# A mixer layer on one core: the Gelu of u held behind the decay chain's last Exp, the gate normalised in pairs, modulation sums called in other slots

## The chip, the cores and the metric

The kernel runs on one core of a Trainium2 chip. Time is device microseconds (us) from one execution of the whole program; lower is better. The engines are TensorE (PE, matmuls; its weight loads are listed as PEld), VectorE (DVE), ScalarE (ACT), GpSimd (POOL) and SyncE (SP, which issues most of the loads). Each engine runs its own list of instructions strictly in order, and waits at an instruction until what it needs is there.

## The reference

One layer over 512 tokens of width 1024, with 256 tokens of context. A wide projection gives u, vs, q, r, ga, gb, k, v and a low-rank input of the decay. Cut to what the change touches:

```python
u, vs, q, r, ga, gb, k, v, lr = _split(h @ w_in, IN_SPLITS)
# spatial gating: vs is layer-normalised over its 1024 channels, mixed over chunks of 128 tokens in 8 groups
a = gelu(u) * (einsum('gpq,bnqgc->bnpgc', w_s, layer_norm(gelu(vs))) + b_s)
# gated linear attention, both directions, 4 heads, chunks of 64 tokens
la = log_sigmoid(lr @ w2 + b2) / 16
b = cumsum(la)            # within a chunk
q_dec, k_inv, k_dec = q * exp(b), k * exp(-b), k * exp(b_last - b)
o = o * rsqrt(mean(o * o) + EPS)      # per head, over 256 channels
ob = o * gla_norm_g * silu(r)
merged = sigmoid(ga) * (a @ w_br_a) + sigmoid(gb) * (ob @ w_br_b)
x = x + g1 * (merged @ w_o)
...                       # then a gated feed-forward block with a 3x3 convolution
```

The vectors g1, sh2, sc2 and g2, by which branches are scaled and shifted, are products of silu(c) with a matrix (w_ada).

## The kernel before

**Matmuls.** Everything is float32. A product is done as three matmuls of rounded halves: high x high, high x low, low x high. A weight comes by DMA into a "raw" tile; ACT's rounding copy makes its high half wh (L152 for whole weights, L232 for sums of weights, whose source is called tt), DVE's subtraction makes its low half wl (L153, L233). Activations are split the same way (L398, L399). Most 128x512 matmuls are at L406 (columns of w_in) and L492 (below).

**Stages, in order, with their place in the profiled execution:** context and heads 0 to 2 (to 189 us); the "u units" (189 to 261); the products VS (vs, 261 to 301), GA (ga, 301 to 353), br_a (a @ w_br_a, 353 to 397), GB (gb, 397 to 438), R (r, 438 to 478), br_b (478 to 531), W_o (531 to 573); the feed-forward part (573 to 931).

**The u units.** For j = 0 to 7, 24 matmuls (L406) give one 128-channel block u_j in a PSUM bank, and `A.activation(ug[j], ps, AF.Gelu)` (L1249) empties it. In each unit `u_slot()` is called twice; it runs the next piece of the attention of heads 2 and 3 (`hook()`). For the last head these pieces are, in order, the decay step `step_z(3)`, the output of head 2 with the sums of its squares (L1050, tiles called junk, read from PSUM banks of the pool "gl"), then `step_transpose` (L978 transposes the context's decayed k, which DVE made at L960; L986 those of the latents), scores, states and outputs.

**step_z.** ACT moves the decay's projections out of PSUM (L912, L880); log-sigmoid is an Exp (L923, for the context L888) and a Ln with bias 1 (L925, L889); DVE makes the running sums over chunks (L931, L892); ACT takes the Exps (L943 to L945, for the context L894); DVE multiplies them with q and k (L956, L957, L960). Where ACT turns from one set of functions to another, the compiled program has an ACT_TABLE_LOAD.

**Strassen products.** `strassen` (from L482) does each of VS, GA, GB, R and W_o as seven half-size products named a11, s3, s2, a12, s1, a22 and s4, of two steps each: 14 slots of 12 matmuls (L492). Between products ACT copies PSUM pairs (L501 after a11, L506 after s3, L510 after s2), and DVE adds pairs (L511, L522). The `step` function that it is given is called once in each slot and puts other work there.

**The gate.** After VS, statistics of gelu(vs) give a scale and an offset for each token; eight ACT instructions (L1287, Identity with bias and scale, 128x512 each) apply them to the eight tiles vr. In GA's step function `ga_step`, `sgu_part(j)` does four small matmuls (L1337) into a bank of the pool "mm", DVE adds the bias (L1339) and multiplies with u_j (L1342); `a_split` then splits u_j for br_a. The two PSUM pools, mm and gl, have four banks each, handed out in turn.

**Modulation sums.** `ada2` is a generator that `tick()` advances; a first group gives g1 and sh2, a second one sc2. Rows of w_ada come in (tiles wa, 256 KB each, on SP's queue), DVE adds them into accumulators (L1307), and at the end of a group a pair of matmuls with ones (L1315, L1316) sums each accumulator over the partitions. In GB, `o_scale` calls `tick()` in each slot.

**What sets the order.** The program is written as one sequence; a scheduler lays it out on the engines by dependencies and its own estimates. `behind(start, name)` (L93) adds an order-only dependency: all instructions traced since `start` come after the one called `name`.

Of the kernel before, what the change touches and what calls it, by code (L numbers as in the profile page):

```python
# [12 lines left out]
AF = mybir.ActivationFunctionType  # L13
# [20 lines left out]
def backbone_kernel(  # L34
# [6 lines left out]
    nc = tc.nc  # L41
    V, A, G, T = nc.vector, nc.scalar, nc.gpsimd, nc.tensor
# [11 lines left out]
    def nm(s):  # L54
        cnt[0] += 1
        return f"{s}_{cnt[0]}"

    def heap(shape, dt=F32, s="h"):
        return hp.tile(shape, dt, tag="h", name=nm(s))
# [18 lines left out]
    def traced():  # L78
        return nc.cur_bb.bb.instructions
# [13 lines left out]
    def behind(start, name):  # L93
        for i in traced()[start:]:
            tc.add_manual_dep(i, name, mybir.DependencyInfo(
                mybir.DependencyClass.NoSync, mybir.DependencyReason.DATA), reason="behind")

    def table_for(func):
        name = [i.name for i in traced() if i.engine == nc.scalar.engine][-1]
        start = len(traced())  # L100
        A.preload_act_table(func)
        behind(start, name)
# [213 lines left out]
    def weights(lead=1, ahead=AHEAD):  # L316
        i = pos[2]
        pos[2] += 1
        stream_split(i + 1 + lead)
        stream_load(i + 1 + ahead)  # L320
        return splits.pop(i)
# [60 lines left out]
    def tick(n=1):  # L382
        for _ in range(n):
            while bg:
                try:
                    next(bg[0])
                    break
                except StopIteration:
                    bg.pop(0)
# [92 lines left out]
    def strassen(acts, done, step, low_first=False):  # L482

        def prod(ps, name, again):
            for j in range(2):
                wh, wl = weights(3, 6)
                for t in range(2):
                    for kk in range(2):
                        ah, al = acts(name, 2 * j + kk, t)
                        first = j == 0 and kk == 0 and not again  # L490
                        for i, (a, b) in enumerate(((ah, wh), (ah, wl), (al, wh))):
                            T.matmul(ps[t], a, b[:, kk, :], start=(first and i == 0),  # L492
                                     stop=(j == 1 and kk == 1 and i == 2), skip_group_check=again)
                step()

        pair = lambda pool: [pool() for _ in range(2)]
        a = pair(mm)
        prod(a, "a11", False)
        b = pair(gl)
        for t in range(2):  # L500
            A.copy(b[t], a[t])  # L501
        e = pair(mm)
        prod(e, "s3", False)
        es = [heap([P, 512], s="es") for _ in range(2)]
        for t in range(2):
            A.copy(es[t], e[t])  # L506
        prod(b, "s2", True)
        c = pair(gl)
        for t in range(2):
            A.copy(c[t], b[t])  # L510
            V.tensor_tensor(b[t], b[t], es[t], op=ALU.add)  # L511

        def c11():
            prod(a, "a12", True)
            for t in range(2):
                done(0, t, a[t], 1.0)

        if not low_first:
            c11()
        prod(c, "s1", True)  # L520
        for t in range(2):
            V.tensor_tensor(es[t], c[t], es[t], op=ALU.add)  # L522
            done(1, 2 + t, es[t], -1.0)
        prod(b, "a22", True)
        for t in range(2):
            done(0, 2 + t, b[t], 1.0)
        if low_first:
            c11()
        prod(c, "s4", True)
        for t in range(2):  # L530
            done(1, t, c[t], -1.0)
# [264 lines left out]
    for k in range(KT):  # L796
# [10 lines left out]
        n = 0  # L807
# [62 lines left out]
    def zc_head(h):  # L870
        S_ = heads[h]
        bcol, wz = gate_col(h)
        zc = gl()
        for d in range(2):
            T.matmul(zc[:, d * LC:(d + 1) * LC], wz[d], lrc, start=True, stop=True)

        lm = wp.tile([P, 4, LC], F32, tag="raw", name=nm("lm"), bufs=5)
        l, m = lm[:, 0:2, :], lm[:, 2:4, :]
        for d in range(2):
            A.activation(l[:, d, :], zc[:, d * LC:(d + 1) * LC], AF.Abs, bias=bcol[d])  # L880
        for d in range(2):
            V.tensor_scalar(m[:, d, :], zc[:, d * LC:(d + 1) * LC], bcol[d], 0.0, op0=ALU.add, op1=ALU.min)
        S_["zc"] = l, m

    def zc_tail(h):
        S_ = heads[h]
        l, m = S_.pop("zc")
        A.activation(l, l, AF.Exp, scale=-1.0)  # L888
        A.activation(l, l, AF.Ln, bias=one_t)  # L889
        for d in range(2):  # L890
            r = slice(None, None, -1 if d == 0 else 1)
            V.tensor_tensor_scan(m[:, d, r], m[:, d, r], l[:, d, r], 0.0, op0=ALU.add, op1=ALU.subtract)  # L892
            G.memset(l[:, d, LC - 1:LC] if d == 0 else l[:, d, 0:1], 1.0)
            A.activation(l[:, d, d:LC - 1 + d], m[:, d, 1 - d:LC - d], AF.Exp, scale=1.0 / 16)  # L894
        S_["ec"] = l
# [5 lines left out]
    def zx_head(h):  # L901
        S_ = heads[h]
        bcol, wz = gate_col(h)
        zx = []
        for d in range(2):
            z = gl()
            T.matmul(z, wz[d], lrx, start=True, stop=True)
            zx.append(z)
        lx, mx = [], []
        for d in range(2):  # L910
            l_ = heap([P, 4, P], s="lx")
            A.activation(l_, zx[d], AF.Abs, bias=bcol[d])  # L912
            m_ = heap([P, 4, P], s="mx")
            V.tensor_scalar(m_, zx[d], bcol[d], 0.0, op0=ALU.add, op1=ALU.min)
            lx.append(l_)
            mx.append(m_)
        S_["zx"] = lx, mx
# [32 lines left out]
    def step_decay(h):  # L950
        S_ = heads[h]
        kx, qx, kc = kxs.pop(h), qxs.pop(h), kcs.pop(h)
        v4 = lambda ap: ap.rearrange("p (i t) -> p i t", i=4)
        S_["q"], S_["k"] = [], []
        for d in range(2):
            V.tensor_tensor(S_["ek"][d], v4(kx), S_["ek"][d], op=ALU.mult)  # L956
            V.tensor_tensor(S_["eq"][d], v4(qx), S_["eq"][d], op=ALU.mult)  # L957
            S_["k"].append(S_["ek"][d])
            S_["q"].append(S_["eq"][d])
        V.tensor_tensor(S_["ec"], S_["ec"], kc.unsqueeze(1).to_broadcast([P, 2, LC]), op=ALU.mult)  # L960

    def mm3(ps, a, b, start, stop):
        for z, (p_, q_) in enumerate(((a[0], b[0]), (a[0], b[1]), (a[1], b[0]))):
            T.matmul(ps, p_, q_, start=(start and z == 0), stop=(stop and z == 2))  # L964

    def step_z(h):
        zx_head(h)
        zc_head(h)
        zx_tail(h)
        zc_tail(h)  # L970
        step_decay(h)

    def step_transpose(h):
# [253 lines left out]
    slots = [0]  # L1227

    def u_slot():
        slots[0] += 1  # L1230
        n = slots[0]
        hook()
        if n == 8:
            sgu_load()
        if n > 8:
            next(summing)
        if n in (11, 13):
            sgu_turn((n - 11) // 2)

    ug = []  # L1240
    for j in range(KT):
        w = weights()
        ps = (mm if j < 3 else gl)()
        for k in range(KT):
            prod_k(ps, w, hx, k, 0, S)
            if k == 3:
                u_slot()
        ug.append(heap([P, S], s="ug"))
        A.activation(ug[j], ps, AF.Gelu)  # L1249
        u_slot()  # L1250
    for low in s3_low:
        low()

    vraw = [[None] * 4 for _ in range(2)]
# [27 lines left out]
    vrs, ors = var[:, 0, :], var[:, 1:5, :]  # L1282
    vnb = const([P, 4], "vnb")
    V.scalar_tensor_tensor(vnb, mv[:, :, 0], -1.0, vrs, op0=ALU.mult, op1=ALU.mult)
    for hf in range(2):
        for t in range(4):
            A.activation(vraw[hf][t], vraw[hf][t], AF.Identity, bias=vnb[:, t:t + 1], scale=vrs[:, t:t + 1])  # L1287

    bc_g = {}
    cols = {}  # L1290
# [53 lines left out]
    def a_split():  # L1344
        a_act.append(split_act(ug[len(a_act)], s="a", eng=A.copy))
# [8 lines left out]

    def ga_step():
        slots[0] += 1
        n = slots[0] - 5
        if 0 <= n < KT:
            sgu_part(n)
        if n >= KT:  # L1360
            a_split()

    strassen(of_sums, ga_done, ga_step)
    slots[0] = 0

    def br_a_done(hf, t, ps):
# [36 lines left out]
    scale_todo = [(t, hf) for hf in range(2) for t in (0, 1, 2, 3)]  # L1403

    def o_scale():
        if scale_todo:
            t, hf = scale_todo.pop(0)
            os_[t][hf] = late([P, 512], s="os")
            for q in range(2):
                h = 2 * hf + q  # L1410
                A.mul(os_[t][hf][:, q * 256:(q + 1) * 256], o_tok[h][t // 2][:, t % 2, :], ors[:, h, t:t + 1])
        tick()

    strassen(of_sums, gb_done, o_scale)
    ada_bank[0] = gl

# [513 lines left out]
    for t in range(2):  # L1930
# [5 lines left out]
        start = len(traced())  # L1936
# [55 lines left out]
```

## Time and profile before

| | |
|---|---|
| median of 3 runs | 933.89 us (933.57 to 934.73) |
| the profiled execution | 932.99 us, of which 931.3 from its first to its last instruction |
| mean granted clock of PE | 0.990 |
| PE, DVE, ACT, POOL busy | 898.0, 766.6, 490.6, 72.0 us |
| HBM read | 135.52 MB |

In the rows of the profile a line reads: start, duration, engine, source line, operation, output<-inputs, shape, how many; in brackets the idle time of the engine before it and what ended that. Rows of stretches give for each engine its busy time in the stretch and the number of instructions that touch it. L-numbers are lines of the kernel before; the changed kernel has the same statements some lines lower (L1249 is L1257 there, L1287 is L1298, L492 is L495).

### The profile page before, as it was taken

The page shows a single profiled execution, that of the slowest core. Times are in us where ns is not written, and L with a number is a line of the kernel's source. Part 1 is how long each engine was busy: PE and PEld are TensorE (multiplying, and loading weights), DVE is VectorE, ACT ScalarE, POOL GpSimd, SP SyncE. Part 2 cuts the span into 40 slices and gives each one's busy share as a digit, 9 for nine tenths or more (in the row PEclk, how much of TensorE's full clock was granted, in tenths as well). Part 3 has the DMA queues.
Part 4 walks back from the last instruction along what each step waited for, and adds up shares of the span by engine and source line. Part 5 has one row for each costly group of instructions (what it writes and reads, how often), then busy time and mean ns, then how long its engine had stood idle before and what let it go on. Part 6 is the DMA issues. An engine that isn't in the chain of part 4 may idle for free.

```text
span 931.3 us, 12864 instructions
## 1 busy us (share of the span) xinstructions
PE 898.0 (96%) x4647; PEld 754.1 (81%) x4647; DVE 766.6 (82%) x1324; ACT 490.6 (53%) x858; POOL 72.0 (8%) x108
## 2 busy tenths in 40 slices
PE   7999999996999799999989999999999999999996
PEld 5777899986888688878868878988888888888885
DVE  5667686876986597888995798799999888999796
ACT  5156464678465762365652568633333343366573
POOL 3000000000121100111111010000000000123000
PEclk9999999998999899999999999999999999999998
DMA  9950401202867548969869074254534333399512
GB/s 271 338 153 1 137 24 46 69 23 78 200 133 206 114 157 258 329 148 305 226 202 226 25 180 138 70 157 130 163 115 125 102 108 108 87 236 261 139 68 91
DMA packets 128093, 138.46 MB, mean 149 GB/s; under 512 B 7401, under 2 KB 84533, under 8 KB 128029
## 3 DMA queue, kind: packets, MB, share of 16 engines
q1 hardware_dynamic: 115933, 117.85, 40.6%
q0 software_dynamic: 10368, 18.57, 11.9%
q10 hardware_dynamic: 1728, 1.22, 0.4%
q8 instruction: 36, 0.59, 0.3%
q14 instruction: 28, 0.23, 0.1%
HBM read 135.52 MB, written 2.10 MB: 148 GB/s over the span
## 4 chain that ended last, share of the span: by engine, by line
PE 78%; DVE 8%; DMA 6%; ACT 5%; issue 1%; SPq 0%; ACTq 0%; POOL 0%; DVEq 0%; POOLq 0%
PE mm L406 27%; PE gl L492 8%; PE gl L1775 6%; PE mm L492 5%; PE mm L1775 4%; PE mm L437 4%; PE mm L430 4%; PE gl L406 4%; DMA wa<-in_w_ada_dram 3%; PE mm L421 2%; PE mm L737 2%; PE gl L964 2%; DMA tt<-in_w_in_dram 2%; PE gl L737 1%; DVE acc L1307 1%
## 5 line engine op out<-in xcount | busy, mean ns | idle before, releaser
L152 ACT CAST wh<-raw 128x1024 fp32r<-128x1024 f32 x110 | 114.3, 1051 | 125.0 <-PE mm L406 67.8
L153 DVE TENSOR_TENSOR wl<-raw,wh 128x1024 fp32r<-128x1024 f32 x110 | 133.3, 1220 | 24.6 <-ACT wh L152 22.2
L1658 DVE SCALAR_TENSOR_TENSOR cacc<-ca,ccol,cacc 128x441 f32<-128x441 f32 (+2 forms) x176 | 121.0, 694 | 6.1 <-ACT cacc L1646 2.8
L406 PE MATMUL mm<-h2h,wh 128*128 128x512 f32 x320 | 124.5, 389 | 0.0
L406 PE MATMUL mm<-h2l,wh 128*128 128x512 f32 x320 | 124.5, 389 | 0.0
L406 PE MATMUL mm<-h2h,wl 128*128 128x512 f32 x320 | 124.5, 389 | 0.0
L406 PEld LDWEIGHTS mm<-h2l,wh 128*128 128x128 f32 x320 | 60.1, 188 | 12.5
L406 PEld LDWEIGHTS mm<-h2h,wh 128*128 128x128 f32 x320 | 60.1, 188 | 12.5
L406 PEld LDWEIGHTS mm<-h2h,wl 128*128 128x128 f32 x320 | 60.1, 188 | 12.3
L232 ACT CAST wh<-tt 128x512 fp32r<-128x512 f32 x60 | 35.4, 620 | 34.8 <-DVE tt L245 15.9
L1307 DVE SCALAR_TENSOR_TENSOR acc<-wa,c_col,acc 128x512 f32<-128x512 f32 x64 | 45.4, 746 | 8.5 <-DMA wa<-in_w_ada_dram 8.3
L1661 ACT ACTIVATE cacc<-cacc 128x512 f32<-128x512 f32 x22 | 13.9, 633 | 61.0 <-DVE cacc L1658 60.9
L233 DVE TENSOR_TENSOR wl<-tt,wh 128x512 fp32r<-128x512 f32 x60 | 39.7, 684 | 5.9 <-ACT wh L232 5.8
L208 POOL DMA_DIRECT2D tt<-in_w_in_dram x32 | 27.5, 927 | 159.4 <-DMA tt<-in_w_in_dram 66.6
L492 PE MATMUL mm<-wh,hxh 128*128 128x512 f32 x96 | 38.0, 395 | 0.0
L492 PE MATMUL mm<-wh,hxl 128*128 128x512 f32 x96 | 37.4, 389 | 0.0
L492 PE MATMUL mm<-wl,hxh 128*128 128x512 f32 x96 | 37.4, 389 | 0.0
L492 PE MATMUL gl<-wh,xh 128*128 128x512 f32 x64 | 26.5, 415 | 5.0 <-ACT gl L501 4.8
L1697 POOL DMA_DIRECT2D b<-in_ffn_w_down_dram x11 | 10.1, 939 | 271.0 <-DMA b<-in_ffn_w_down_dram 257.4
L1717 ACT CAST wh<-raw 128x1024 fp32r<-128x1024 f32 x22 | 23.0, 1052 | 15.3 <-PE mm L1775 4.4
L1718 DVE TENSOR_TENSOR wl<-raw,wh 128x1024 fp32r<-128x1024 f32 x22 | 26.8, 1219 | 4.5 <-ACT wh L1717 4.3
L492 PE MATMUL gl<-wl,xh 128*128 128x512 f32 x64 | 25.5, 399 | 0.0
(534 smaller groups left out, 2461.1 us busy)
## 6 DMA issues: line engine op xcount, KB each, us to landing
raw<-in_w_in_dram SPq DMA_DIRECT2D x54, 512.0 KB, 5.2
wa<-in_w_ada_dram SPq DMA_DIRECT2D x96, 256.0 KB, 5.8
raw<-in_ffn_w_up_dram SPq DMA_DIRECT2D x44, 512.0 KB, 3.9
raw<-in_ffn_w_down_dram SPq DMA_DIRECT2D x22, 512.0 KB, 3.4
tt<-in_w_in_dram POOLq DMA_DIRECT2D x32, 256.0 KB, 6.9
tt<-in_w_in_dram SPq DMA_DIRECT2D x16, 256.0 KB, 4.9
raw<-in_w_br_a_dram SPq DMA_DIRECT2D x8, 512.0 KB, 3.5
raw<-in_w_br_b_dram SPq DMA_DIRECT2D x8, 512.0 KB, 5.3
```

Source lines behind the costliest of these rows:

```text
L152: A.copy(wh, raw)
L153: low = lambda: V.tensor_tensor(wl, raw, wh.bitcast(F32), op=ALU.subtract)
L232: A.copy(wh[:, kk, :], tt[j][kk])
L233: V.tensor_tensor(wl[:, kk, :], tt[j][kk], wh[:, kk, :].bitcast(F32), op=ALU.subtract)
L406: T.matmul(ps, a[:, k, :], b[:, c0:c0 + n], start=(k == 0 and i == 0), stop=(k == KT - 1 and i == 2))
L430: T.matmul(ps, a[:, t * P:(t + 1) * P], b[:, k % 4, :], start=(k == 0 and i == 0), stop=(k == KT - 1 and i == 2))
L437: T.matmul(ps, a, b[:, k % 2, :], start=(k == 0 and i == 0), stop=(k == KT - 1 and i == 2))
L492: T.matmul(ps[t], a, b[:, kk, :], start=(first and i == 0), stop=(j == 1 and kk == 1 and i == 2), skip_group_check=again)
L737: T.matmul(fps[i], a, b, start=(k == 0 and z == 0), stop=(k == KT - 1 and z == 2))
L1307: V.scalar_tensor_tensor(a_, w_, c_col[:, k:k + 1], a_, op0=ALU.mult, op1=ALU.add)
L1658: V.scalar_tensor_tensor(o, a_[:, r0 + dy:r1 + dy, c0 + dx:c1 + dx], wcol(tap), o, op0=ALU.mult, op1=ALU.add)
L1775: T.matmul(ps, a[:, t * P:(t + 1) * P], w[b][:, j, c0:c0 + n], start=(first and i == 0), stop=(last and i == 2), skip_group_check=again)
```

## The change

1. In `step_z` the name of ACT's last instruction so far, the context's last Exp, is kept in `last_exp`. The Gelu of each u_j gets an order-only dependency on it, and the second `u_slot()` of a unit is called ahead of the Gelu. For heads before the last, the dependency is on an Exp that is long past.
2. The eight normalisations leave their place after VS. `vs_norm(i)` does two of them, behind ACT's latest instruction; `ga_step` calls it in slots 3 to 6. `sgu_part` comes one slot later (slots 6 to 13 in place of 5 to 12), `a_split` in slot 14 and once after GA.
3. `o_scale` calls `tick()` in GB's slots 1 to 4 and 9 to 12 alone.

```diff
@@ -95,8 +95,11 @@
             tc.add_manual_dep(i, name, mybir.DependencyInfo(
                 mybir.DependencyClass.NoSync, mybir.DependencyReason.DATA), reason="behind")
 
+    def last_of(engine):
+        return [i.name for i in traced() if i.engine == engine.engine][-1]
+
     def table_for(func):
-        name = [i.name for i in traced() if i.engine == nc.scalar.engine][-1]
+        name = last_of(nc.scalar)
         start = len(traced())
         A.preload_act_table(func)
         behind(start, name)
@@ -963,11 +966,14 @@
         for z, (p_, q_) in enumerate(((a[0], b[0]), (a[0], b[1]), (a[1], b[0]))):
             T.matmul(ps, p_, q_, start=(start and z == 0), stop=(stop and z == 2))
 
+    last_exp = [None]
+
     def step_z(h):
         zx_head(h)
         zc_head(h)
         zx_tail(h)
         zc_tail(h)
+        last_exp[0] = last_of(nc.scalar)
         step_decay(h)
 
     def step_transpose(h):
@@ -1245,9 +1251,11 @@
             prod_k(ps, w, hx, k, 0, S)
             if k == 3:
                 u_slot()
+        u_slot()
         ug.append(heap([P, S], s="ug"))
+        start = len(traced())
         A.activation(ug[j], ps, AF.Gelu)
-        u_slot()
+        behind(start, last_exp[0])
     for low in s3_low:
         low()
 
@@ -1282,9 +1290,13 @@
     vrs, ors = var[:, 0, :], var[:, 1:5, :]
     vnb = const([P, 4], "vnb")
     V.scalar_tensor_tensor(vnb, mv[:, :, 0], -1.0, vrs, op0=ALU.mult, op1=ALU.mult)
-    for hf in range(2):
-        for t in range(4):
-            A.activation(vraw[hf][t], vraw[hf][t], AF.Identity, bias=vnb[:, t:t + 1], scale=vrs[:, t:t + 1])
+
+    def vs_norm(i):
+        name, start = last_of(nc.scalar), len(traced())
+        for t in (2 * (i % 2), 2 * (i % 2) + 1):
+            v_ = vraw[i // 2][t]
+            A.activation(v_, v_, AF.Identity, bias=vnb[:, t:t + 1], scale=vrs[:, t:t + 1])
+        behind(start, name)
 
     bc_g = {}
     cols = {}
@@ -1354,13 +1366,16 @@
 
     def ga_step():
         slots[0] += 1
-        n = slots[0] - 5
+        n = slots[0] - 6
+        if -3 <= n <= 0:
+            vs_norm(n + 3)
         if 0 <= n < KT:
             sgu_part(n)
         if n >= KT:
             a_split()
 
     strassen(of_sums, ga_done, ga_step)
+    a_split()
     slots[0] = 0
 
     def br_a_done(hf, t, ps):
@@ -1403,14 +1418,17 @@
     scale_todo = [(t, hf) for hf in range(2) for t in (0, 1, 2, 3)]
 
     def o_scale():
+        slots[0] += 1
         if scale_todo:
             t, hf = scale_todo.pop(0)
             os_[t][hf] = late([P, 512], s="os")
             for q in range(2):
                 h = 2 * hf + q
                 A.mul(os_[t][hf][:, q * 256:(q + 1) * 256], o_tok[h][t // 2][:, t % 2, :], ors[:, h, t:t + 1])
-        tick()
-
+        if slots[0] < 5 or 8 < slots[0] < 13:
+            tick()
+
+    slots[0] = 0
     strassen(of_sums, gb_done, o_scale)
     ada_bank[0] = gl
```

The following rows are the engines' instruction lists, before and after; the number behind a tile's name tells its buffers apart.

ACT in the u units, before: from the load ahead of the second unit's Gelu to the first squares. lx, mx and lm are the decays of the latents (two directions) and of the context, dec their values at the chunks' ends, ug a Gelu result, junk the squares of head 2's output:

```order
L1249 ACT_TABLE_LOAD
L1249 ACTIVATE ug_2481<-mm_2456 128x512
L943 ACT_TABLE_LOAD
L943 ACTIVATE dec_2417<-dec_2417 128x4
L944 ACTIVATE mx_2395<-lx_2393 128x512
L943 ACTIVATE dec_2429<-dec_2429 128x4
L944 ACTIVATE mx_2399<-lx_2397 128x512
L945 ACTIVATE lx_2393<-lx_2393 128x512
L945 ACTIVATE lx_2397<-lx_2397 128x512
L889 ACT_TABLE_LOAD
L889 ACTIVATE lm_2404<-lm_2404,one_t 128x512
L1050 ACTIVATE junk_2494,oss<-gl_2483 128x256
```

After, from the first Exp of the sums to the first squares:

```order
L946 ACTIVATE dec_2415<-dec_2415 128x4
L947 ACTIVATE mx_2393<-lx_2391 128x512
L892 ACTIVATE lm_2402<-lm_2402,one_t 128x512
L948 ACTIVATE lx_2391<-lx_2391 128x512
L946 ACTIVATE dec_2427<-dec_2427 128x4
L947 ACTIVATE mx_2397<-lx_2395 128x512
L897 ACTIVATE lm_2402<-lm_2402 128x255
L948 ACTIVATE lx_2395<-lx_2395 128x512
L897 ACTIVATE lm_2402<-lm_2402 128x255
L1257 ACT_TABLE_LOAD
L1257 ACTIVATE ug_2448<-mm_2308 128x512
L1056 ACTIVATE junk_2492,oss<-gl_2481 128x256
```

The Gelu and the loads are gone from between the Exps; one load stands behind the last Exp (the second L897), and the squares, which stood ahead of the last Exp, stand behind it and behind the first Gelu.

ACT in GA, before, from the first copy of a11's pair (L501) to the first copy of s3's pair (L506); "..." leaves out five like rows of vr:

```order
L501 COPY gl_3451<-mm_3404 128x512
L232 CAST wh_3460<-tt_3317 128x512
L1287 ACTIVATE vr_3232<-vr_3232,vnb,var 128x512
L1287 ACTIVATE vr_3235<-vr_3235,vnb,var 128x512
...
L1287 ACTIVATE vr_3284<-vr_3284,vnb,var 128x512
L501 COPY gl_3452<-mm_3405 128x512
L152 CAST wh_3480<-raw_3412 128x1024
L506 COPY es_3496<-mm_3455 128x512
```

After, from the second copy (L504) on:

```order
L504 COPY gl_3444<-mm_3397 128x512
L1298 ACTIVATE vr_3232<-vr_3232,vnb,var 128x512
L1298 ACTIVATE vr_3235<-vr_3235,vnb,var 128x512
L155 CAST wh_3474<-raw_3404 128x1024
L1298 ACTIVATE vr_3334<-vr_3334,vnb,var 128x512
L1298 ACTIVATE vr_3337<-vr_3337,vnb,var 128x512
L509 COPY es_3492<-mm_3447 128x512
L155 CAST wh_3496<-raw_3429 128x1024
L509 COPY es_3493<-mm_3448 128x512
L1298 ACTIVATE vr_3378<-vr_3378,vnb,var 128x512
L1298 ACTIVATE vr_3381<-vr_3381,vnb,var 128x512
L155 CAST wh_3516<-raw_3344 128x1024
```

The second copy has moved ahead of the normalisations, which stand in pairs between weight halves (L155) and copies (L509).

DVE in GA, before, from the first low half of a12's weight on:

```order
L153 TENSOR_TENSOR wl_3481<-raw_3412,wh_3480 128x1024
L1339 SCALAR_TENSOR_TENSOR mm_3518<-mm_3518,vec_b,sgb_2686 128x512
L153 TENSOR_TENSOR wl_3501<-raw_3437,wh_3500 128x1024
L1342 TENSOR_TENSOR ug_2387<-mm_3518,ug_2387 128x512
L153 TENSOR_TENSOR wl_3526<-raw_3344,wh_3525 128x1024
L1339 SCALAR_TENSOR_TENSOR mm_3543<-mm_3543,vec_b,sgb_2686 128x512
L511 TENSOR_TENSOR gl_3451<-gl_3451,es_3496 128x512
L1342 TENSOR_TENSOR ug_2481<-mm_3543,ug_2481 128x512
L511 TENSOR_TENSOR gl_3452<-gl_3452,es_3497 128x512
```

After:

```order
L156 TENSOR_TENSOR wl_3475<-raw_3404,wh_3474 128x1024
L156 TENSOR_TENSOR wl_3497<-raw_3429,wh_3496 128x1024
L156 TENSOR_TENSOR wl_3517<-raw_3344,wh_3516 128x1024
L514 TENSOR_TENSOR gl_3443<-gl_3443,es_3492 128x512
L514 TENSOR_TENSOR gl_3444<-gl_3444,es_3493 128x512
L1351 SCALAR_TENSOR_TENSOR mm_3536<-mm_3536,vec_b,sgb_2684 128x512
L156 TENSOR_TENSOR wl_3550<-raw_3364,wh_3549 128x1024
L1354 TENSOR_TENSOR ug_2448<-mm_3536,ug_2448 128x512
```

Two more low halves and both sums (L514, before L511) now stand ahead of the first bias addition (L1351, before L1339).

PE in GB, before, the first pair with ones:

```order
L492 MATMUL gl_4228<-wl_4199,xh_2876 128x512
L492 MATMUL gl_4228<-wh_4198,xl_2877 128x512
L1315 MATMUL mm_4311<-acch_4191,ones_r 128x512
L1316 MATMUL mm_4311<-accl_4192,ones_r 128x512
L492 MATMUL gl_4227<-wh_4236,xh_2958 128x512
```

After:

```order
L495 MATMUL gl_4333<-wl_4312,xh_2874 128x512
L495 MATMUL gl_4333<-wh_4311,xl_2875 128x512
L1327 MATMUL mm_4402<-acch_4191,ones_r 128x512
L1328 MATMUL mm_4402<-accl_4192,ones_r 128x512
L495 MATMUL gl_4332<-wh_4338,xh_2956 128x512
```

The pair stands some 48 matmuls further on; gl_4228 and gl_4333 are PSUM banks of two different products.

## Prediction

> **What bounds the kernel now.** I read the busy shares first, then the waits of TensorE (PE), then the granted clock around its long waits, then the timelines of ScalarE (ACT) and VectorE (DVE) just ahead of them.
>
> ```profile
> span 931.3 us, 12864 instructions
> PE 898.0 (96%) x4647; PEld 754.1 (81%) x4647; DVE 766.6 (82%) x1324; ACT 490.6 (53%) x858; POOL 72.0 (8%) x108
> ```
>
> PE is busy for 898.0 of 931.3 us and the change takes no matmul away, so it can pay only in PE's waits and in the slow clock that follows them. The waits by what ended them, for 185 to 262 us and then for 262 to 600 us (columns: total, times, longest):
>
> ```profile
> PE gl L978 <- DVE lm L960: 7.1, 1, 7.1
> ...
> PE gl L492 <- ACT gl L501: 4.8, 1, 4.8
> ...
> PE mm L1315 <- ACT es L506: 0.9, 1, 0.9
> ```
>
> The first lies in the u units, the second in the product GA, the last in GB. Each part of the change sits just ahead of one of the three; the two rows left out are waits at the head of br_b, which it leaves alone. The clock around the two long waits (the number behind POOL's count is the granted clock):
>
> ```profile
> 218.00:222.00 4.00, 1.97 (x9) 1.98 (x10) 0.74 (x2) 3.96 (x9) 0.00 (x0) 0.50 0.00 0
> 222.00:226.00 4.00, 4.00 (x19) 3.41 (x19) 2.81 (x4) 4.00 (x6) 0.00 (x0) 0.84 0.55 144
> ...
> 318.00:322.00 4.00, 3.90 (x11) 3.22 (x12) 1.23 (x1) 4.00 (x7) 0.00 (x0) 0.50 0.53 92
> ```
>
> [...] In the u units that costs 2 us x 0.5 + 4 us x 0.16 = 1.6 us on top of the 7.1.
>
> **Part 1, the Gelu of u behind the decay chain.** In the u units ACT is the engine that is late. First its whole stretch, then its rows and DVE's:
>
> ```profile
> 196.90:219.20 22.30, 16.00 (x88) 13.48 (x86) 14.31 (x37) 22.09 (x38) 0.20 (x2) 0.94 0.00 1
> 205.90:219.98 14.08, 9.49 (x25) 0.87 0.00 0
> ...
> 196.99 1.28 ACT L1249 ACT_TABLE_LOAD   x1
> 198.29 0.60 ACT L1249 ACTIVATE ug<-mm 128x512 f32<-128x512 f32 x1
> 205.16 1.34 ACT L925 ACTIVATE lx<-lx,one_t 128x512 f32<-128x512 f32 x2
> 216.31 0.37 ACT L1050 ACTIVATE junk<-gl 128x256 bf16<-128x256 f32 x1
> 216.67 0.38 ACT L1050 ACTIVATE junk<-gl 128x256 bf16<-128x256 f32 x1
> 212.51 0.39 PE L406 MATMUL mm<-hxh,wl 128*128 128x512 f32 x1
> 220.03 1.11 PE L978 MATMUL gl<-ident,lm 128*128 128x128 f32 x4 [7.13 <-DVE lm L960]
> ```
>
> ACT is busy for 22.09 of the 22.30 us that end with the last Exp (L894). Nine table loads stand in the u units, of 1.28 us each; the changed order has one. Eight of them, 10.3 us, lie ahead of the last Exp. Three loads (3.85 us) and a Gelu stand ahead of the Ln pair (L925), so that pair starts at 205.16 - 3.85 - 0.5 = 200.8; I take 201.6, since the projections ahead of it (L912, L880) wait for PE and DVE. Its first half is done at about 202.3. From there DVE carries the chain: in the stretch from its first scan to the end of L960 it has 9.49 us of work, so L960 ends at about 202.3 + 9.5 = 211.8. PE comes to L978 right behind the L406 that starts at 212.51, at about 212.7. So the 7.13 us wait goes whole, with 0.9 us to spare, and the half clock with it.
>
> What is late next is the squares of the head before (L1050), which stand behind the one load and the first Gelus in the new order. They read the PSUM banks that L978, L986 and the fourth unit's matmuls want. ACT's last Exp ends at about 209.4 (it runs some 2.3 us ahead of L960, whose inputs L956 and L957 DVE still has to make); then the load (1.30 from its row to the next), two Gelus (0.60 less the overlap, 0.5 each), four squares (0.36 each from start to start) and one wh copy (0.94, from rows in part 2) end at 209.4 + 1.3 + 1.0 + 1.45 + 0.95 = 214.1, and the bank is free at about 214.2. PE has ten transposes to do from 212.74 (four took 1.11 us at half clock, so by an estimate ten take 1.3 at full clock), and so wants the bank at 214.0: 0.2 us of wait. Term: -(7.1 + 1.6) + 0.2 = -8.5. Bounds: -8.7, if nothing new waits, and -6.5, if L960 or the squares come 2 us later than I reckon. The Gelu results themselves are read only in GA; u0, u1 and u2 stay in three banks of a pool of four, and the order has u3 in the other pool.
>
> [...]
>
> **Part 2, the normalisation of the gate in pairs.** ACT ahead of the wait in GA, then DVE behind it:
>
> ```profile
> 311.82 5.75 ACT L1287 ACTIVATE vr<-vr,vnb,var 128x512 f32<-128x512 f32 x8 [0.15 <-DVE vnb L1284]
> 317.48 0.57 ACT L501 COPY gl<-mm 128x512 f32<-128x512 f32 x1
> ...
> 317.99 1.03 ACT L152 CAST wh<-raw 128x1024 fp32r<-128x1024 f32 x1
> 318.93 1.05 ACT L506 COPY es<-mm 128x512 f32<-128x512 f32 x2
> 318.10 0.80 PE L492 MATMUL gl<-wh,xh 128*128 128x512 f32 x1 [4.83 <-ACT gl L501]
> 326.31 0.40 PE L492 MATMUL mm<-wl,hxh 128*128 128x512 f32 x1
> 328.59 0.39 PE L492 MATMUL mm<-wh,hxl 128*128 128x512 f32 x1
> 328.82 1.05 PE L1337 MATMUL mm<-swT,vr 128*128 128x128 f32 x8
> 329.63 0.48 PE L492 MATMUL mm<-wh,hxh 128*128 128x512 f32 x1
> 333.25 0.48 PE L492 MATMUL gl<-wh,xh 128*128 128x512 f32 x1
> ...
> 319.06 1.23 DVE L153 TENSOR_TENSOR wl<-raw,wh 128x1024 fp32r<-128x1024 f32 x1 [6.66 <-ACT wh L152]
> 322.90 0.76 DVE L1339 SCALAR_TENSOR_TENSOR mm<-mm,vec_b,sgb 128x512 f32<-128x512 f32 x1 [2.62 <-ACT wh L152]
> 324.70 0.68 DVE L1342 TENSOR_TENSOR ug<-mm,ug 128x512 f32<-128x512 f32 x1
> ```
>
> The eight normalisations (5.75 us) stand between the two copies L501 (the first is done ahead of them), and the second copy is what PE waits for. In the new order the second copy follows the first closely, at about 312, ahead of PE's need: the wait begins at 318.10 - 4.83 = 313.27, and since a matmul overlaps the next by 0.16 (0.39 long, 0.228 from start to start: ten of them from 326.31 to 328.59), the next one was due at 313.1. So these 5.0 us go. Between 318.10 and 333.25 PE does 42 matmuls of 0.228 and four gate products of 0.81 (328.82 to 329.63): 9.6 + 3.2 = 12.8 us of work in 15.15, so the slow clock took 2.35. Gross: 5.0 + 2.35 = 7.3.
>
> A wait comes in its place. The third gate product (L1337) wants the PSUM bank that DVE's L1342 of the first one frees. In the new order DVE has L1339 of the first product behind two sums L511, and these wait for copies (L510) that stand behind the last normalising pair on ACT. By 0.71 for a normalisation, 0.48 for a copy and 0.94 for a wh copy, and none of them before its input is there, ACT reaches L510 at 321.6 and 322.1; then DVE, with 0.6 to 0.7 for each of the half-width steps and 1.15 for an L153: both L511 to 323.45, L1339 to 324.1, L153 to 325.25, L1342 to 325.9. PE, without a wait, is there at 313.1 + 42 x 0.228 + 2 x 0.81 = 324.3. New wait: 1.6. Following DVE's new order on at the same pitches, the later products find their banks free (the fourth wants L1342 done at 328.4 and comes at 329.5; the seventh wants 331.5 and comes at 340.1). The gate products come one slot later each, and one slot without them is left ahead of br_a, as against two before, so their inputs to br_a are not late. Term: -7.3 + 1.6 = -5.7. Bounds: -7.3, no wait, and -3.5, the wait twice as long and a shorter one behind it.
>
> Ahead of this, in VS, two subtractions (L233) now stand behind an L243 that waits for a transfer:
>
> ```profile
> 288.51 1.23 DVE L243 TENSOR_TENSOR raw<-raw,raw 128x1024 f32<-128x1024 f32 x1 [5.74 <-DMA raw<-in_w_in_dram]
> 294.14 0.68 DVE L522 TENSOR_TENSOR es<-gl,es 128x512 f32<-128x512 f32 x1
> 295.43 0.39 PE L492 MATMUL gl<-wh,s4h 128*128 128x512 f32 x1
> ```
>
> They come out of idle time and go into a full stretch, so the sum L522 at 294.14 is 1.2 us later, against 0.6 us of slack (it ends at 294.8, and PE's matmul on that bank starts at 295.4). Term: +0.5, bounds 0 and +1.5.
>
> **Part 3, the modulation sums.** Four pairs of small matmuls (L1315, L1316) move from GB's slots 5 to 8 to slots 9 to 12. The first of them waited 0.9 us for a copy (L506) that stood late on ACT; four slots later that copy is done. Term: -0.9; bounds -1.1 and 0. The next group's loads (256 KB each, on SP's queue) and its VectorE sums then come later, and more of them fall into R, where the transfers are already dense (the last two numbers are the DMA share and GB/s):
>
> ```profile
> 430.00:440.00 10.00, 10.00 (x46) 8.29 (x45) 7.76 (x11) 4.15 (x7) 0.59 (x1) 1.00 1.09 285
> ```
>
> Four to six loads more are 1.0 to 1.5 MB, at 285 GB/s 3.7 to 5.5 us of transfer. R's weights are fetched some 10 us or more ahead of their use, and a pair of them now stands behind two raw loads on SP's queue, 5 to 6 us later. On my count they land 2 us before PE wants them. Term: 0; bounds -0.3 (a short wait of PE at 460 goes) and +5.
>
> **Sum.** -8.5 + 0.5 - 5.7 - 0.9 + 0 = -14.6. All behind GB (br_b, W_o, the feed-forward part) is PE-bound and only moves ahead. The profiled execution took 932.99 us, so 918.4; the median of the runs is 0.9 above it, so 919.3.
>
> **Rivals.** A: nothing new waits; the bounds -8.7, 0, -7.3, -1.1, -0.3 give -17.4, 916.5. For it: VS and the third gate product turn on 0.5 and 1.6 us read out of an order of instructions. Against it: the L1342 chain above has no slack in any step.
> B: R becomes bound by its transfers (+5) or the u units keep 2 us of wait and VS takes 1.5: -14.6 + 5 = -9.6, or -14.6 + 2 + 1 = -11.6; 922 to 924.5. For it: the share of 1.09. Against: no wait of PE on a DMA stands in the list above.
> C, the slower side: the wait for the gate's bank is not once but in every slot. DVE is the engine that is full there, and L1339 of each product stands behind two other operations. Six more slots at the same 1.6 give +9.6, 928.9. It ends slower than before only if each of these six costs over 14.6 / 6 = 2.4 us. Against: the banks by my count are free 1.1 us ahead and more.
> D: the Gelu's move does nothing for PE, since L960 is held by DVE and not by ACT. Then 9.5 us of DVE work would have to start no earlier than 205.9; but it starts when the Ln pair is done, and 3.85 us of loads ahead of that are gone. At most half of the term is lost: 923.5.
>
> **How the numbers follow.** Forecast (917.5 to 922): 0.62. A: 0.14. B: 0.12. D: 0.06. C: 0.06, half of it slower than before. The range 916.3 to 924.7 leaves out C, a part of D and of A. A difference under 0.2% (1.9 us) can't be told from none here. Faster 0.94 (all but C's tail), same 0.03, slower 0.03.
>
> **What would show it.** In the profile after: one table load in the u units and no PE wait on L960; in the list of waits a wait of 1 to 2 us for a bank on the third gate product; none between the two L501 copies; the granted clock at 1.00 from 210 to 330; GB's wait on L506 gone; br_b starting about 14.6 us sooner. I am wrong if PE shows new waits on DVE through GA, or on transfers in R.

## The result and the profile after

The changed kernel took 919.16 us in the median of 6 runs (917.96 to 920.22), the kernel before 933.73 us in the 6 runs made beside them (932.07 to 935.47): a ratio of 0.9844, 95% interval 0.9829 to 0.9858. That is 14.6 us less. The profiled execution has a span of 917.6 us, 13.7 less than the one shown of before.

Two lines of the page after, and PE's waits from 262 to 600 us; for 150 to 262 us the same view has no line left:

```profile
span 917.6 us, 12867 instructions
...
PE 895.8 (98%) x4647; PEld 751.8 (82%) x4647; DVE 766.0 (83%) x1324; ACT 479.3 (52%) x850; POOL 71.9 (8%) x108
...
PE gl L1402 <- DVE sr L1442: 3.0, 1, 3.0
PE mm L495 <- DVE wl L156: 0.9, 2, 0.6
PE mm L1402 <- DVE sr L1442: 0.4, 1, 0.4
PE gl L495 <- DVE es L525: 0.4, 1, 0.4
PE gl L495 <- DVE wl L156: 0.3, 1, 0.3
```

ACT has eight instructions and 11.3 us less (490.6 to 479.3), 10.3 of them the eight table loads. The waits on L960, L501 and L506 are gone. What has come in their place lies in R and at the head of br_b: L1402 (L1387 before) waits for VectorE's L1442, and four small waits precede it.

Where the time went is read from the start of the same matmul in both traces: the first L406 of the fifth unit, the first L492 of GA, GB, R and W_o. The gain of each stretch, in us (negative is faster), for the changed kernel and for four of the experiments below:

| stretch | before, us | changed | parts 1+2 | part 3 | part 1 | part 2 |
|---|---|---|---|---|---|---|
| start to fifth unit | 231.41 | -9.23 | -8.81 | +1.14 | -9.28 | +1.25 |
| to GA (VS) | 69.46 | 0.00 | +0.01 | 0.00 | +0.02 | +0.86 |
| GA and br_a, to GB | 95.95 | -6.83 | -7.09 | +0.47 | -2.24 | -5.41 |
| GB, to R | 41.21 | -1.21 | -1.21 | -1.21 | +0.05 | -1.21 |
| R and br_b, to W_o | 93.64 | +3.62 | -0.15 | +3.44 | +0.62 | -1.03 |
| W_o to the end | 399.60 | -0.04 | -0.04 | -0.04 | +0.09 | -0.04 |

Of the first -9.23, 0.56 is there before the first changed instruction (the L406 matmuls from 100 us on start that much sooner); it is no part of the change, which leaves 8.67. Of the +3.62, 2.4 lies within R (39.98 to 42.35). The rest lies behind it, at the head of br_b, where the changed kernel waits 3.05 us and then has 3.41 us of half clock (467.75 to 471.17); the kernel before waits 1.79 and 1.33 us there, without any half clock.

The rows of the u units after, ACT and DVE ahead of the transposes, then PE:

```profile
200.75 1.33 ACT L928 ACTIVATE lx<-lx,one_t 128x512 f32<-128x512 f32 x2
207.58 0.40 ACT L897 ACTIVATE lm<-lm 128x255 f32<-128x255 f32 x1
208.00 1.28 ACT L1257 ACT_TABLE_LOAD   x1
209.29 0.60 ACT L1257 ACTIVATE ug<-mm 128x512 f32<-128x512 f32 x1
212.77 0.40 ACT L1056 ACTIVATE junk<-gl 128x256 bf16<-128x256 f32 x1
...
209.57 0.69 DVE L963 TENSOR_TENSOR lm<-lm,kc 128x512 f32<-128x512 f32 x1
...
212.19 0.60 PE L984 MATMUL gl<-ident,lm 128*128 128x128 f32 x4
213.31 0.50 PE L409 MATMUL gl<-hxh,wh 128*128 128x512 f32 x1
```

L963 (L960 before) is done at 210.26, PE comes at 212.19 and does not wait. The last squares end at about 213.2, and the fourth unit starts at 213.31, right behind the ten transposes and with no wait: the bank came just in time.

GA after, ACT, DVE and PE at the third gate product, and VectorE's wait for a transfer in VS:

```profile
300.99 0.58 ACT L504 COPY gl<-mm 128x512 f32<-128x512 f32 x1
301.51 1.51 ACT L1298 ACTIVATE vr<-vr,vnb,var 128x512 f32<-128x512 f32 x2
310.96 1.06 ACT L513 COPY gl<-gl 128x512 f32<-128x512 f32 x2
...
314.57 0.68 DVE L1354 TENSOR_TENSOR ug<-mm,ug 128x512 f32<-128x512 f32 x1
315.40 1.13 PE L1349 MATMUL mm<-swT,vr 128*128 128x128 f32 x8
...
276.97 1.23 DVE L246 TENSOR_TENSOR raw<-raw,raw 128x1024 f32<-128x1024 f32 x1 [5.47 <-DMA raw<-in_w_in_dram]
```

The second copy ends ahead of PE's need. L1354 of the first product frees the bank at 315.25, and the third product starts at 315.40; PE's lead over the trace of before shrinks by 0.26 us at this place.

### The profile page after: what moved, and what is told of

It is laid out like the page before. It is cut to its first block, busy times and chain, and to the rows that moved or that the text cites. A ratio compares the mean times of both kernels' runs of the same rounds, so it can differ in the third digit from the quotient of the medians.

```text
span 917.6 us, 12867 instructions
## 1 busy us (share of the span) xinstructions
PE 895.8 (98%) x4647; PEld 751.8 (82%) x4647; DVE 766.0 (83%) x1324; ACT 479.3 (52%) x850; POOL 71.9 (8%) x108
## 4 chain that ended last, share of the span: by engine, by line
PE 76%; DVE 11%; DMA 5%; ACT 4%; issue 3%; POOL 0%; SPq 0%; ACTq 0%; DVEq 0%; POOLq 0%
PE mm L409 28%; PE gl L1793 6%; PE gl L495 5%; PE mm L1793 4%; PE mm L440 4%; PE mm L433 4%; PE gl L409 4%; PE mm L495 4%; PE gl L967 3%; PE mm L424 3%; PE mm L740 2%; DMA wa<-in_w_ada_dram 2%; DVE wl L156 2%; DMA tt<-in_w_in_dram 2%; DVE acc L1319 1%
## 5 line engine op out<-in xcount | busy, mean ns | idle before, releaser
L155 ACT CAST wh<-raw 128x1024 fp32r<-128x1024 f32 x110 | 114.5, 1050 | 112.8 <-PE mm L409 68.5
L409 PE MATMUL mm<-hxh,wl 128*128 128x512 f32 x64 | 25.1, 392 | 0.3 <-DVE wl L156 0.3
```

The lines of the kernel that those rows point to most:

```text
L155: A.copy(wh, raw)
L409: T.matmul(ps, a[:, k, :], b[:, c0:c0 + n], start=(k == 0 and i == 0), stop=(k == KT - 1 and i == 2))
```

## The experiments

All are against the kernel before, run beside them. Theory T holds that the 3.6 us lost in R and br_b come from part 3; its rival S, that R cannot follow because all ahead of it comes sooner.

**Parts 1 and 2 without part 3** (`o_scale` as before, `tick()` in every slot):

```diff
-        if slots[0] < 5 or 8 < slots[0] < 13:
-            tick()
+        tick()
```

> Parts 1 and 2 of the change alone; GB's step function calls the modulation sums as before. Theory T (the 3.65 us that the changed kernel loses in R come from part 3: modulation sums that now fall into R on VectorE, and a pair of tt loads issued later): the loss goes, GB's wait of 0.9 us (1.2 us with its margin) comes back: 919.2 - 3.65 + 1.2 = 916.7 us, first matmul of br_b at least 15 us sooner than in the kernel before. Rival S (R loses because everything ahead of it comes 17 us sooner and its transfers cannot follow): the loss stays, 919.2 + 1.2 = 920.4 us, with waits of PE in R as in the changed kernel.

915.55 us, ratio 0.9813 (0.9796 to 0.983). T holds: R and br_b take 0.15 us less than before, though R starts 17 us sooner. GB's wait did not come back, which no theory had: GB gains the same 1.21 us. The copy L506 that PE waited for starts at 393.26 here, with GB 15.89 us sooner, and at 410.87 before: 1.7 us sooner against PE.

**Part 3 alone:**

> Part 3 of the change alone, on the kernel before. T: GB gains 1.2 us and R loses 3.65: 933.7 + 2.4 = 936.1 us, slower than before by 0.26%. S: GB's gain alone, 932.5 us.

937.26 us, ratio 1.0046 (1.0029 to 1.0063): slower than before. The loss in R and br_b is 3.44 us and the gain in GB 1.21, as T has it. The first row of the table is 1.14 us off with nothing changed there; see the last section.

**Part 1 alone and part 2 alone:**

> Part 1 alone (the Gelus of u behind the last Exp). Both theories: the wait on L960 and the slow clock behind it go, -8.7 us, 925.0 us; the 4.8 us wait on the second L501 copy stays. In VS the transfer that VectorE waits for should come some 2 us sooner against PE than in the kernel before, as in the changed kernel, if that is part 1's doing.

> Part 2 alone (the normalisations in pairs). If the third gate product finds its bank almost free whatever the u units do: -6.8 us, 926.9 us. If it did so in the changed kernel only because part 1 brings a transfer in VS 2.3 us sooner against PE, then here the wait of 1.6 us that was forecast shows on the third gate product and VS loses up to 0.5 us: -5.7 + 0.5, 928.5 us.

Part 1: 922.08 us, ratio 0.9883 (0.9861 to 0.9905). Part 2: 925.46 us, ratio 0.9921 (0.9903 to 0.994). The lines that tell them apart: part 1's wait and its row of VectorE in VS, then the same of part 2:

```profile
PE gl L495 <- ACT gl L504: 3.0, 1, 3.0
276.55 1.23 DVE L246 TENSOR_TENSOR raw<-raw,raw 128x1024 f32<-128x1024 f32 x1 [5.10 <-DMA raw<-in_w_in_dram]
...
PE gl L981 <- DVE lm L963: 7.1, 1, 7.1
PE mm L1344 <- DVE ug L1349: 1.4, 1, 1.4
290.96 1.23 DVE L246 TENSOR_TENSOR raw<-raw,raw 128x1024 f32<-128x1024 f32 x1 [6.92 <-DMA raw<-in_w_in_dram]
```

With part 2 alone the wait on the gate's bank is there, 1.4 us, and VS loses 0.86: the two terms that the prediction had and the changed kernel did not show. What hid them is part 1. Measured from the first matmul of VS, VectorE gets its transfer at 27.84 us before and at 29.01 with part 2 alone, but at 25.52 in the changed kernel and at 25.14 with part 1 alone (288.51 - 260.67, 290.96 - 261.95, 276.97 - 251.45, 276.55 - 251.41). So in the changed kernel the transfer came 2.3 us sooner against PE than before, and at the end of VS VectorE still had 1.4 us of this: the instruction that makes the gate's offsets (vnb) started at 301.03 as against 311.62, 10.6 us sooner where PE was 9.2, and ACT's chain in GA starts with them. By the same shift part 1 alone shortens GA's wait from 4.8 to 3.0 us and gains 2.24 us there, most of the 2.9 us by which it falls below its forecast. Why part 1's order brings this transfer forward isn't shown; it isn't that PE comes sooner, for with seven table loads put back (the last experiment), when PE reaches the fifth unit as late as before, the transfer still comes at 25.26 (285.96 - 260.70). GB's gain belongs to part 2 as well as to part 3: each brings it alone.

The time of part 2, 925.46 us, is below both of its forecasts. Its trace is of an execution that took 927.41, the longest of four.

**What in part 3 costs the time.** The difference in R: VectorE's modulation sums in R, before and after (stretch, its length, busy time of these sums alone and their number), then all of VectorE's work in R's full stretch, and the rows where it stands idle ahead of it:

```profile
438.03:478.01 39.98, 7.12 (x10) 1.00 0.71 210
420.77:463.12 42.35, 10.67 (x15) 1.00 0.70 201
...
446.00:478.01 32.01, 30.75 (x45) 1.00 0.66 190
428.30:463.12 34.82, 33.69 (x50) 1.00 0.69 202
...
425.70 0.62 ACT L235 CAST wh<-tt 128x512 fp32r<-128x512 f32 x1 [8.49 <-DMA tt<-in_w_in_dram]
426.35 0.69 DVE L236 TENSOR_TENSOR wl<-tt,wh 128x512 fp32r<-128x512 f32 x1 [4.75 <-ACT wh L235]
```

R has five sums more, 3.55 us of VectorE, and VectorE is full (33.69 of 34.82 us) once it starts; and it starts late, since the second pair of tt loads lands late. The loads of wa for these sums have moved too. Three theories, V (the sums), Q (the queue order of the tt loads) and D (the transfers as such):

The sums left out, the loads kept (`if kinds != ("sc",):` ahead of the sum in `ada2`):

> The changed kernel, without VectorE's 16 sums of the last modulation group (sc): its loads stay where they are, the sums are left out, so the shift and scale vectors of the second norm are not the reference's. V (VectorE has too much to do in R, some 0.67 us for each sum): 10.7 us of work go from R, PE's waits there go and the 3 us at the head of br_b shrinks: 919.2 - 3.65 - up to 2 = 913.5 to 915.5 us. Q (the second pair of tt loads stands behind two raw loads on SP's queue, lands late and leaves VectorE idle for 4.75 us): the idle time stays, half of the loss or more stays, 917 to 919 us. D (16 loads of 256 KB fill the transfers): nothing changes, 919 us.

The loads left out but two, the sums kept in their places:

```diff
-                w_ = late([P, 512], s="wa2")
-                dma(w_, ...)
+                if kinds != ("sc",) or k == 0:
+                    w_ = late([P, 512], s="wa2")
+                    dma(w_, ...)
```

> The changed kernel, with the 16 sums of that group in their places but only the first two of its 16 loads made (the sums read the second tile again and again, so the result is not the reference's). V: the loss in R stays, 918 to 919.2 us. Q: the pair of tt loads is issued as late as before, its transfer is faster, 917 to 919 us, with the idle time of VectorE near 4 us. D: the loss goes, 915.5 us.

The tt loads first:

```diff
 def load_b12(j):
     def load():
+        start = len(traced())
         load_raw("b12", 0, 1, j)()
+        if c0 == O_R:
+            behind(start, last_load["tt"])
```

> The changed kernel, with R's two b12 raw loads ordered behind the second pair of tt loads on SP's queue, nothing left out; 15 of the 16 sums still stand in R. Q: VectorE's idle stretch of 4.75 us ahead of R shrinks by about 5 us of earlier issue, and most of the loss goes: 916 to 917 us. V: VectorE is as full as in the changed kernel, but starts on R up to 2.8 us sooner, since what it does is spread over a longer stretch: 917.5 to 919 us. D: 919 us.

The times and ratios, and the change from the first matmul of R to that of W_o against the changed kernel's 97.26 us. Each ratio is to the kernel before, run beside it on the same chip, so kernels are best compared by these; the changed kernel's is 0.9844 (0.9829 to 0.9858):

| run | median, us | ratio to before (95%) | R and br_b |
|---|---|---|---|
| no sums | 912.74 | 0.9795 (0.9781 to 0.9809) | -6.46 |
| no loads | 915.79 | 0.983 (0.9816 to 0.9843) | -2.57 |
| tt first | 917.92 | 0.9847 (0.9834 to 0.9861) | -0.41 |

V holds for the greater part: without the sums the ratio falls clear of the changed kernel's, and R and br_b are even 2.8 us shorter than before the change. The loads have a part as well. Without them all 16 sums stand in R, so V forecast no gain, and yet R and br_b are 2.57 us shorter; the time, 915.79, is what D had forecast. This second part is the weaker one: the ratio lies within the changed kernel's interval, and the 2.57 comes from one trace, of an execution that took 918.26, the longest of four. Nor is D the whole, for with the loads gone PE still waits 3.1 us at the head of br_b. PE's longest waits for these banks:

```profile
PE gl L1403 <- DVE sr L1445: 0.8, 1, 0.8
...
PE gl L1403 <- DVE sr L1443: 3.1, 1, 3.1
...
PE gl L1406 <- DVE sr L1446: 3.1, 1, 3.1
PE mm L1406 <- DVE sr L1446: 1.3, 1, 1.3
```

(The lines are of no sums, no loads and tt first.) Putting the tt loads first cures nothing: the ratio is that of the changed kernel within the intervals, and PE waits as long at the head of br_b. It doesn't refute Q outright. VectorE's idle time of 4.75 us shrinks to 3.02, but it then waits three times for loads of wa, so that its waits in R come to 7.6 us as against 6.5; and 13 of the sums stand in R, not 15. What the loads cost beside the sums, by their bandwidth or by the order that they force on SP's queue, stays open.

**The sums held behind R.** If VectorE's load in R is the cause, the cure leaves nothing out: an order-only dependency of these 16 sums on VectorE's last instruction of R. First on parts 1 and 2, with `tick()` in GB's slots 1 to 8, then as the one edit on the changed kernel:

```diff
+                start = len(traced())
                 V.scalar_tensor_tensor(a_, w_, c_col[:, k:k + 1], a_, op0=ALU.mult, op1=ALU.add)
+                if kinds == ("sc",) and r_end[0]:
+                    behind(start, r_end[0])
...
     strassen(of_sums, r_done, r_step)
+    r_end[0] = last_of(nc.vector)
```

> Parts 1 and 2, GB's step function calls the modulation sums in its slots 1 to 8 alone, and the 16 sums of the sc group are ordered behind VectorE's last instruction of R (nothing left out). V: R has none of these sums, as against 10 in the run with parts 1 and 2 alone (915.6 us), so the 2 us wait at the head of br_b goes: 913.5 to 914.5 us, if br_b takes 9 us more on VectorE without PE waiting. Against: 16 sums in a row at the head of br_b delay the low halves of br_b's weights, 916 to 919 us.

> The changed kernel with the one edit that the 16 sums of the sc group stand behind VectorE's last instruction of R; GB's slots as changed, nothing left out. V: as the run with that edit and GB's slots 1 to 8, 912.7 us, at most 1.5 us more where the tt loads are late. If the order of the tt loads mattered by itself (Q): 914 to 916 us.

912.67 us, ratio 0.979 (0.9777 to 0.9804), and 912.07 us, ratio 0.9772 (0.9757 to 0.9787). The second is the fastest kernel of this study, 21 us below the kernel before; by the ratios it is 0.7% below the changed kernel. Its whole list of PE waits from 190 to 600 us, and VectorE in br_b up to W_o (all its work, then the sums alone):

```profile
PE mm L495 <- DVE wl L156: 0.6, 1, 0.6
...
461.80:511.40 49.60, 44.74 (x71) 1.00 0.66 179
461.80:511.40 49.60, 10.93 (x16) 1.00 0.66 179
```

br_b takes the 10.93 us of sums without a wait of PE, though VectorE is busy there for 44.74 of 49.60 us. So the price of a sum depends on the stage. In R, where VectorE makes seven products' weights and sums PE's results, 15 sums (10.67 us) and what came with them cost 7.6 us (97.26 to 89.64, the half clock at the head of br_b among them); in br_b 16 sums cost no wait. The sums don't move alone, for a held sum keeps its buffer and so holds back later loads: of the 16 loads, eight are issued in R in the changed kernel, at 430 to 438 us; with the sums held it is six, at 443 to 459 us, and three more behind R. This cure shows what to do, and not how much of the loss was the sums' and how much the loads'.

**Were the table loads the cause in the u units?** Part 1 moved the Gelus, the squares and eight loads at once. Here all of ACT's work keeps its new place but two wh copies, and loads come back: one or three forced ahead of the Ln pair, and the compiler then adds four:

```diff
+        if h == NH - 1:
+            for func in (AF.Gelu,):        # second run: (AF.Gelu, AF.Sqrt, AF.Gelu)
+                table_for(func)
         for t_ in lx:
             A.activation(t_, t_, AF.Ln, bias=one_t)
```

> The changed kernel with one table load for Gelu forced between the Exp and the Ln of the last head's decay; the compiler then puts four more loads (ahead of the Ln pair, of the context's Exp, of its Ln and of the next Exp), 5 x 1.28 = 6.4 us, and nothing else is moved but two wh copies of ACT that now stand behind the squares. If the loads were what part 1 saved: L963 ends 2.6 to 5.1 us later than its 210.3 us, PE (there at 212.4) waits again, and the squares (4.5 us later than now) hold the fourth unit's bank: a wait of about 4 us in all, 923 us, up to 924.6 with the slow clock behind it. If it was the order of the Gelus and squares that counted and not the loads: 919.2 us.

> The same with two loads more (seven, 9.0 us), ahead of the Ln pair. Loads: 2.6 us more than the run with five, an idle time of PE of 6 to 7 us, so half clock behind it as in the kernel before: 926 to 928 us. Order: 919.2 us.

925.39 us, ratio 0.9918 (0.9895 to 0.994), and 926.27 us, ratio 0.9921 (0.9905 to 0.9938). PE at the transposes, with five loads and with seven, and the clock behind each:

```profile
215.93 1.11 PE L987 MATMUL gl<-ident,lm 128*128 128x128 f32 x4 [4.00 <-DVE o L1057]
218.00:222.00 4.00, 4.00 (x13) 3.19 (x12) 3.83 (x5) 4.00 (x6) 0.00 (x0) 0.62 0.91 280
...
218.99 1.11 PE L987 MATMUL gl<-ident,lm 128*128 128x128 f32 x4 [6.57 <-ACT junk L1059]
222.00:226.00 4.00, 4.00 (x16) 3.27 (x15) 3.00 (x4) 3.07 (x5) 0.00 (x0) 0.69 0.93 317
```

The loads are the cause: with five the fifth unit starts 6.0 us later than in the changed kernel, with seven 9.3, which is as late as before, though the Gelus and the squares keep their new places. Two loads (2.57 us) cost 2.57 us of wait. VectorE's last step of the chain ends at 215.22 and 218.29, as against 210.26; what PE waits for last is what follows it, copies of head 2's output (L1057) and its squares (L1059). Both times are clear of the changed kernel's, but they don't part from each other: the four with five loads spread from 923.95 to 928.49.

These runs also show why two Gelus in the chain came with eight loads. The kernel loads one table at its start (L129 of the changed kernel, at 0.80 us of its trace). No other load stands there until the one ahead of the Gelu at 208.00, so after the change the Exp, Ln, Exp of this chain need none. In the run with five loads the forced one, for Gelu, starts at 200.45, and four more of 1.28 us stand behind it, ahead of a Ln (L931, at 201.74), an Exp (L891, 204.39), a Ln (L892, 207.90) and an Exp (L951, 209.93). In the trace of before, two loads for the Gelus (196.99 and 208.44) and six for Exps and Lns stand from 196.99 to 217.16.

## Why the prediction was right, and where it was not

The time was forecast at 919.3 us and came at 919.16; the terms did not all come as forecast. Their sum was -14.6; the same places measure -13.7 between the traces, 0.56 of which is not the change's, which leaves -13.1. The medians differ by 14.6.

- **u units: -8.5 forecast, -8.67 measured.** The steps held: the Ln pair (forecast 201.6, measured 200.75 in a trace that runs 0.56 us sooner), L960's end (211.8; 210.26), the squares as the next to be late (0.2 us of wait forecast, none seen). The two runs with loads put back show the same chain from the other side.
- **VS: +0.5 forecast, 0 measured; GA: -5.7 forecast, -6.83 measured.** One step failed for both: VectorE's place in VS was kept at its distance from PE in the trace of before, while the transfer that it waits for came 2.3 us sooner against PE. Both waits exist (0.86 and 1.4 us with part 2 alone), and the cover came from part 1. The 1.6 us of bank wait came as 0.26.
- **GB: -0.9 forecast, -1.21 measured**, but put down to part 3 alone. Parts 1 and 2 bring it without part 3.
- **R: 0 forecast, +3.6 measured**, inside the bounds of -0.3 and +5. This is the step that failed. The prediction named the sums that fall into R, but priced the loads alone; five sums more, 3.55 us on an engine that was full, were not in the sum, and the two waits at the head of br_b, which the prediction took as left alone (1.79 and 1.33 us), became one of 3.05 us with half clock behind it. That 3.55 and 3.6 are so near is no proof: the loss holds a half clock too, and without the loads 2.57 us of it went. Rival B had the size, with the transfers as its cause; PE still waits for no DMA, as was held against B, but the run without loads leaves the transfers a part by way of VectorE.
- **The half clock.** The prediction put it at 1.6 and 2.35 us behind the two long waits. In the trace of before it ended 3.25 and 4.17 us after PE went on (at 223.28 and 322.27), so 1.6 and 2.1 us; what sets its end isn't shown.
- **Rival A** (nothing new waits, 916.5) has about the time that parts 1 and 2 alone take, 915.55, though PE waits 2.0 us at the head of br_b there. **C** did not come: the bank wait shows once, even with part 2 alone. **D** is out: L963 is done 1.9 us ahead of PE.

So 1.6 us more gained in VS and GA, 0.3 in GB, and 3.6 lost in R. By the traces the sum misses by 1.5 us; that the median came within 0.2 us of the forecast is luck. The mechanism held for the u units and for the wait on the second copy in GA; it did not for VS, for who brings GB's gain, and for R.

## What to carry to other kernels

Before a change moves work off a waiting place, add up the receiving stage on each engine: here the one that was busy 31 of 32 us lost time, and the next one, busy 45 of 50 us with the same sums in it, lost none. A wait read out of a new order holds only as long as what feeds it keeps its distance; a part of the same change further ahead can move that. On ScalarE, count the table loads that the compiled program has in a dependent chain: here one forced load for a foreign function brought four more behind it, of 1.28 us each.

## What the runs showed of the hardware

- In the trace of before, the granted clock was 0.50 from 216.46 to 223.28 us and from 315.44 to 322.27, 6.83 us each time; the two starts lie 98.99 us apart, 29 times 3.413. In that of the changed kernel it was 0.50 from 467.75 to 471.17, 3.41 us. Elsewhere from 100 to 900 us both traces have 1.00. In the 3.41 us ahead of these three starts PE stood idle for 3.41, 2.17 and 2.43 us.
- The length of a wait alone did not tell whether half clock followed it. At the head of br_b, with parts 1 and 2, a wait of 1.99 us was followed by half clock, and one of 1.79 us before the change was not. The wait of 3.05 us there in the changed kernel was followed by it, and one of 3.0 us with five loads was not. What decides it isn't shown. The stretches behind these waits, of the changed kernel, of parts 1 and 2, of before and of five loads:

```profile
468.00:472.00 4.00, 4.00 (x13) 3.15 (x13) 4.00 (x7) 0.86 (x2) 0.00 (x0) 0.60 0.76 285
...
464.00:468.00 4.00, 4.00 (x16) 3.37 (x15) 4.00 (x7) 1.17 (x2) 0.00 (x0) 0.67 0.88 279
...
480.00:484.00 4.00, 3.60 (x19) 2.98 (x20) 4.00 (x7) 2.23 (x5) 0.00 (x0) 1.00 0.89 266
...
472.00:476.00 4.00, 4.00 (x21) 3.31 (x22) 4.00 (x7) 2.07 (x5) 0.00 (x0) 1.00 0.74 228
```

- With part 2 alone PE waits 7.1 us ahead of the transposes, as before the change, and yet its fifth unit starts 1.25 us later than in the trace of before; with part 3 alone, which changes nothing there, it starts 1.14 us later. The mean granted clock of one kernel differs from execution to execution: 0.985 to 0.991 in those of the kernel before that were run beside the experiments. The trace of part 3 alone has 0.986 and that of before 0.990; that the half clock behind the 7.1 us wait makes the 1.14 and 1.25 us is an estimate from these figures.
